# Every eighth block of a dense expert pass multiplied whole in float32, in place of a three-term product of two rounded parts

## The chip, the cores and the metric

The kernel runs on one core of one Trainium2 chip. The metric is the device time of one execution in microseconds. The core has a matrix engine (TensorE, PE in the profile, its weight loads PEld), a vector engine (VectorE, DVE), a scalar engine (ScalarE, ACT), GpSimd (POOL, which here mostly issues gathers), and SyncE (SP, which here issues nearly all plain transfers, in order). Each engine works through its own instructions in order and waits for the others by semaphores.

## The reference

One decoder block over 512 tokens of 1024 channels: two gated token mixers, a product-key expert layer (PEER), a gate with per-layer embeddings and a final norm. Only the expert layer matters here. Each token chooses 128 of 16384 experts (8 heads, 16 each):

```python
hid = jax.nn.gelu(jnp.einsum('td,thkd->thk', xb, tab_u[idx]))
return jnp.einsum('thk,thkd->td', gate * hid, tab_v[idx])
```

## The kernel before

Tokens are four tiles of 128. For tiles 0 and 1 the chosen rows of `tab_u` and `tab_v` are gathered one expert slot at a time (`Rows`, 128 rows of 4 KB in one indirect transfer) and worked on VectorE: a dot product at L789, a weighted addition into the tile at L793. Tiles 2 and 3 (`DENSE`, 256 tokens together) are done densely. A first pass (`products_of`, L904) multiplies the tokens with all 16384 experts in 128 blocks of 128 and leaves gate times gelu, a float32 matrix of 128 experts by 256 tokens a block, in `wide_w`; `place_of_block(j)` is the place of block j. A second pass, from about 1393 us on, multiplies these with the rows of `tab_v`: for block j a tile V of 128 experts by 1024 channels is loaded, and the product is added into four accumulators `acc[a, dh]` (two token tiles, two halves of the channels), each of 128 by 512, which stay in PSUM over all blocks.

The second pass is the one that matters. For block j, `split(j)` loads V by SP (L1054) and makes two parts of it and of the weights w: `Vh` (ACT, L1058) is V rounded to the reduced float32 type F32R, `Vl` (DVE, L1059) is the rest, also in F32R; `wh` (ACT, L1060) and `wl` (DVE, L1061) likewise, both in `w_parts`. `values(j, a)` then adds wh·Vh, wh·Vl and wl·Vh for each half: 2 x 3 x 2 = 12 matmuls a block on L1068, each of 128 by 128 weights and 512 moving columns.

What sets the order of the work:

- V has four places in turn: two buffers of the tag `V` (blocks with j % 4 of 0 and 1), and the rows of tiles 2 and 3 of `h` (j % 4 of 2 and 3), which are parked in DRAM for the pass (`rest`) and brought back at L1172. A place is used again four blocks on. SP issues the loads in order of j, so that a load that waits for its place holds back the loads behind it.
- `Vh` and `Vl` have two buffers each, taken in turn. `w_parts` has two places, by the parity of j.
- The four splitting instructions of a block are pinned to program order on ACT and DVE, and so are the gathers of `rows(PB)`: 0.96 expert rows a block of tile 1, each a gather from POOL (L762, five ring buffers `g`) and an addition on DVE (L793).
- Between the blocks, the last projection of the finished tiles is woven in: `finish(t, ...)` with its matmuls at L1094 (`pp`), L1102 and L1112 (`pg`). Its weights (`plew`, four loads of 1280 KB at L1147, and `fgain`, L1145) go into parts of `wide_w` that are no longer needed, and its other loads are at L1088.
- Blocks 126 and 127 are multiplied at the end, and the accumulators are added to `h` at L1179. What comes after that is the rest of `finish`.

In the trace the instructions of L1058 can be counted off from block 0 at 1392.53 us; block 71 is at 1598.81 us and block 119 at 1759.70 us. Float32 matmuls stand in the trace as two records each (2048 on L904 for 128 x 8 matmuls), F32R ones as one.

Of the kernel before, what the change touches and what calls it, by code (L numbers as in the profile page):

```python
# [60 lines left out]
def tile_block(ctx: ExitStack, tc: tile.TileContext, x, smalls, bvec, w1, w2, wbr, wout, wq, wup, gup, subk,  # L61
# [19 lines left out]
    def hrows(t):  # L81
        return first_h if t == 0 else later["h"][:, t - 1, :]
# [7 lines left out]
    def rank(n):  # L90

        tc.cur_priority = int(100000 * n)
# [127 lines left out]
    def pin(ins):  # L220

        return tc.keep_in_program_order(ins)
# [647 lines left out]
    def stream(name, tag):  # L870
        return dense.tile([128, D], F32, name=name, tag=tag, bufs=VS)
# [6 lines left out]
    def place_of_block(j):  # L878
        return wide_w[0][:, j, :] if j < N0 else wide_w[1][:, j - N0, :]
# [169 lines left out]
    halves_of = {}  # L1049

    def split(j):
        rank(9.5 + 0.001 * j)
        V = stream("V", "V") if j % 4 < 2 or j > 125 else hrows(j % 4)
        sp.dma_start(V, V3[:, j, :])  # L1054
        Vh = dense.tile([128, D], F32R, name="Vh", tag="uV", bufs=2)
        Vl = dense.tile([128, D], F32R, name="Vl", tag="X", bufs=VS)
        w, wh, wl = place_of_block(j), w_parts[:, j % 2, 0], w_parts[:, j % 2, 1]
        pin(act.activation(Vh, V, AF.Copy))  # L1058
        pin(dve.tensor_tensor(Vl, V, Vh, op=OP.subtract))  # L1059
        pin(act.activation(wh, w, AF.Copy))  # L1060
        pin(dve.tensor_tensor(wl, w, wh, op=OP.subtract))  # L1061
        halves_of[j] = wh, wl, Vh, Vl

    def values(j, a):
        wh, wl, Vh, Vl = halves_of[j]
        for q, (w, V) in enumerate(((wh, Vh), (wh, Vl), (wl, Vh))):
            for dh in range(2):
                pe.matmul(acc[a, dh], lhsT=w[:, a * 128:(a + 1) * 128], rhs=V[:, dh * 512:(dh + 1) * 512],  # L1068
                          start=j == 0 and q == 0, stop=j == 127 and q == 2)
# [62 lines left out]

    ends = {}
    split(0)
    for j in range(128):
        if j < 127:
            split(j + 1)
        rank(9.5 + 0.001 * j)
        rows(PB)
        if j < 126:  # L1140
            for a in range(2):
                values(j, a)
# [25 lines left out]
    for a in range(2):  # L1168
        for j in (126, 127):
            values(j, a)  # L1170
# [64 lines left out]
```

## Time and profile before

| what | value |
| --- | --- |
| median of 3 runs | 1846.44 us (1845.05 to 1847.0) |
| the profiled execution: its own time | 1847.93 us |
| its span | 1846.2 us |
| PE, DVE, ACT, POOL busy, share of the span | 90%, 78%, 35%, 43% |
| second pass, first matmul of L1068 to the last | 1393.9 to 1792.6 us |

The span is the time between the first and the last instruction of the profiled execution. The times that a row gives for a matmul include its way through the array; matmuls follow one another more closely than that, so that the cost of one is read from the distance between starts, or from a chain that names a run of them with its total.

### The profile page before, as it was taken

Reading aid. Unit: us, or ns where it says so; the run is one execution under the profiler, and the core shown is the slowest. Engines: PE = TensorE matmul, PEld = TensorE weight load, DVE = VectorE, ACT = ScalarE, POOL = GpSimd, SP = SyncE. Lnnn points to the kernel's source line nnn. Section 1 sums busy time; section 2 is a strip of 40 time slices with the busy share of each in tenths; the row PEclk is TensorE's granted clock in tenths of the full one; section 3 lists DMA queues with packets and bytes.
Section 4 is the critical chain, followed back from the end, with each engine's and each line's share of the span. In section 5 each row is a group of like instructions: output and inputs, shape, how many; then the busy total and the mean of one; then the engine's idle time right before and its main releaser. Section 6 shows DMA issues by size and latency. Waiting matters only on the chain.

```text
span 1846.2 us, 26873 instructions
## 1 busy us (share of the span) xinstructions
PE 1659.5 (90%) x9367; PEld 1481.7 (80%) x9367; DVE 1437.5 (78%) x3195; ACT 642.1 (35%) x1456; POOL 801.4 (43%) x608
## 2 busy tenths in 40 slices
PE   7999888999999889949970799999999999999997
PEld 6998878999898878948860689998887777888886
DVE  4532887887878899988627788988998999998773
ACT  3311233233222324401110454544433444454443
POOL 1000344343355465763004666655564554664220
PEclk9999988999999999979995899999999999999999
DMA  8257658556678987994430699999999999999750
GB/s 308 81 168 266 229 188 285 189 182 201 199 248 301 342 311 271 318 382 148 156 128 0 238 380 387 385 376 360 368 370 350 407 393 400 378 367 329 231 172 34
DMA packets 141851, 499.62 MB, mean 271 GB/s; under 512 B 15694, under 2 KB 20884, under 8 KB 141204
## 3 DMA queue, kind: packets, MB, share of 16 engines
q0 software_dynamic: 73728, 268.47, 40.0%
q1 hardware_dynamic: 67328, 228.09, 34.4%
q8 instruction: 74, 1.21, 0.3%
q10 hardware_dynamic: 660, 1.35, 0.2%
q14 instruction: 61, 0.50, 0.1%
HBM read 494.70 MB, written 3.15 MB: 270 GB/s over the span
## 4 chain that ended last, share of the span: by engine, by line
PE 53%; DVE 14%; issue 11%; DMA 11%; POOL 8%; ACT 1%; POOLq 0%; DVEq 0%; ACTq 0%; SPq 0%
PE S L904 14%; PE acc L1068 10%; POOL g L762 5%; PE z L273 5%; DMA g<-in_peer_u_dram,idx 5%; DMA g<-in_peer_v_dram,idx 3%; PE pg L1112 3%; PE pgate L273 3%; PE Z L458 2%; DVE g L789 2%; PE TT L465 2%; POOL sel L729 2%; DVE w L256 2%; PE pq L273 2%; PE cb L988 1%
## 5 line engine op out<-in xcount | busy, mean ns | idle before, releaser
L904 PE MATMUL S<-uT,U 128*128 128x256 f32 x2048 | 459.0, 383 | 26.5 <-ACT w L916 23.6
L762 POOL DMA_INDIRECT g<-in_peer_v_dram,idx x241 | 354.3, 1470 | 294.1 <-DVE h L793 223.2
L904 PEld LDWEIGHTS S<-uT,U 128*128 128x128 f32 x2048 | 388.1, 192 | 78.2 <-ACT w L916 24.0
L762 POOL DMA_INDIRECT g<-in_peer_u_dram,idx x235 | 298.9, 1272 | 248.9 <-DVE g L789 185.2
L793 DVE SCALAR_TENSOR_TENSOR h<-g,coef,h 128x1024 f32<-128x1024 f32 x241 | 308.3, 1279 | 15.1 <-DMA g<-in_peer_v_dram,idx 14.4
L789 DVE SCALAR_TENSOR_TENSOR g<-g,u 128x1024 f32<-128x1024 f32 x235 | 281.8, 1222 | 40.0 <-DMA g<-in_peer_u_dram,idx 39.4
L1068 PE MATMUL acc<-Vh,w_parts 128*128 128x512 f32 x1024 | 285.4, 397 | 5.6 <-ACT w_parts L1060 3.3
L1068 PEld LDWEIGHTS acc<-Vh,w_parts 128*128 128x128 f32 x1024 | 193.0, 189 | 50.3 <-ACT w_parts L1060 5.4
L1068 PE MATMUL acc<-Vl,w_parts 128*128 128x512 f32 x512 | 161.6, 397 | 1.7 <-DVE Vl L1059 1.7
L729 POOL TENSOR_TENSOR sel<-sel 128x800 f32<-128x800 bf16 x32 | 60.2, 1898 | 181.0 <-DVE sel L728 164.3
L1068 PEld LDWEIGHTS acc<-Vl,w_parts 128*128 128x128 f32 x512 | 96.3, 190 | 26.0 <-DVE Vl L1059 5.4
L273 PE MATMUL z<-xh,w 128*128 128x384 f32 x416 | 91.3, 364 | 17.4 <-DVE w L256 8.7
L1058 ACT ACTIVATE Vh<-V 128x1024 fp32r<-128x1024 f32 x66 | 70.0, 1061 | 96.8 <-PE acc L1068 73.6
L1059 DVE TENSOR_TENSOR Vl<-V,Vh 128x1024 fp32r<-128x1024 f32 x66 | 80.8, 1224 | 21.6 <-ACT Vh L1058 21.5
L1058 ACT ACTIVATE Vh<-h 128x1024 fp32r<-128x1024 f32 x62 | 65.8, 1061 | 89.1 <-PE acc L1068 73.2
L273 PEld LDWEIGHTS z<-xh,w 128*128 128x128 f32 x416 | 78.4, 202 | 22.2 <-DVE w L256 9.5
L1059 DVE TENSOR_TENSOR Vl<-h,Vh 128x1024 fp32r<-128x1024 f32 x62 | 76.0, 1226 | 19.1 <-ACT Vh L1058 19.0
L1000 ACT ACTIVATE w<-cb 128x156 f32<-128x156 f32 (+36 forms) x95 | 22.6, 271 | 174.6 <-DVE w L998 171.5
L916 ACT ACTIVATE w<-S 128x256 f32<-128x256 f32 (+41 forms) x123 | 38.1, 314 | 112.0 <-PE S L904 109.4
L988 PEld LDWEIGHTS cb<-h 128*128 128x128 f32 x512 | 67.8, 191 | 10.6 <-ACT h L983 4.0
L988 PE MATMUL cb<-h 128*128 128x128 f32 x512 | 70.1, 277 | 4.7 <-ACT h L983 2.5
L983 ACT ACTIVATE h<-near,gain 128x128 f32<-128x128 f32 x128 | 63.2, 493 | 4.3
(343 smaller groups left out, 2881.0 us busy)
## 6 DMA issues: line engine op xcount, KB each, us to landing
U<-in_peer_ut_dram SPq DMA_DIRECT2D x128, 512.0 KB, 6.3
V<-in_peer_v_dram SPq DMA_DIRECT2D x66, 512.0 KB, 6.5
h<-in_peer_v_dram SPq DMA_DIRECT2D x62, 512.0 KB, 6.4
w1b<-in_w_dram SPq DMA_DIRECT2D x52, 512.0 KB, 5.2
w2m<-in_w_dram SPq DMA_DIRECT2D x32, 512.0 KB, 4.4
wqb<-in_wq_dram SPq DMA_DIRECT2D x32, 512.0 KB, 5.1
wbr<-in_wbr_dram SPq DMA_DIRECT2D x16, 512.0 KB, 4.5
wo<-in_wout_dram SPq DMA_DIRECT2D x16, 512.0 KB, 5.5
```

The costliest lines, as they stand in the source:

```text
L273: pe.matmul(p, lhsT=a(c), rhs=b(c), start=k + c == 0, stop=(k, c) == (len(terms) - 1, n - 1))
L729: pool.tensor_tensor(hit, eq, ci[:, hd, None, :].to_broadcast([128, 16, NCAND]), op=OP.mult)
L762: fetch = pool.indirect_dma_start(out=g, out_offset=None, in_=tab, in_offset=bass.IndirectOffsetOnAxis(ap=ix[:, k:k + 1], axis=0))
L789: done = dve.scalar_tensor_tensor(g, g, 1.0, self.u, op0=OP.mult, op1=OP.mult, accum_out=self.dots[:, hd, k:k + 1])
L793: done = dve.scalar_tensor_tensor(h, g, self.cf[:, k:k + 1], h, op0=OP.mult, op1=OP.add)
L904: done = pe.matmul(p, lhsT=U[:, c * 128:(c + 1) * 128], rhs=uT[c // 4][:, c % 4, :], start=c == 0, stop=c == KC - 1)
L983: pin(act.activation(B[:, q], near, AF.Relu, scale=of(self.minus), bias=of(self.gate)))
L988: pin(pe.matmul(self.p[:, q, :], lhsT=As[:, t4 % 2, q], rhs=Bs[:, t4 % 2, q], start=True, stop=True))
L1058: pin(act.activation(Vh, V, AF.Copy))
L1059: pin(dve.tensor_tensor(Vl, V, Vh, op=OP.subtract))
L1068: pe.matmul(acc[a, dh], lhsT=w[:, a * 128:(a + 1) * 128], rhs=V[:, dh * 512:(dh + 1) * 512], start=j == 0 and q == 0, stop=j == 127 and q ...
L1112: pe.matmul(p[:, :256], lhsT=hT[:, c, :], rhs=plew_s[qd][:, c, :], start=(c == 0), stop=(c == KC - 1))
```

## The change

Blocks with j % 8 == 7 below 126 (7, 15, ..., 119: fifteen of the 128) are not split. Their w and V stay float32 tiles, and one float32 product takes the place of the three F32R products. The accumulators and all other blocks are as they were.

```diff
@@ def split(j):
         rank(9.5 + 0.001 * j)
         V = stream("V", "V") if j % 4 < 2 or j > 125 else hrows(j % 4)
         sp.dma_start(V, V3[:, j, :])
+        if j % 8 == 7 and j < 126:
+            halves_of[j] = place_of_block(j), V
+            return
         Vh = dense.tile([128, D], F32R, name="Vh", tag="uV", bufs=2)
@@ def values(j, a):
-        wh, wl, Vh, Vl = halves_of[j]
-        for q, (w, V) in enumerate(((wh, Vh), (wh, Vl), (wl, Vh))):
+        terms = [halves_of[j]]
+        if len(terms[0]) == 4:
+            wh, wl, Vh, Vl = terms[0]
+            terms = [(wh, Vh), (wh, Vl), (wl, Vh)]
+        for q, (w, V) in enumerate(terms):
             for dh in range(2):
```

## Rows read from the trace of the kernel before

**Rows 1.** Page, part 2: the span in 40 slices, busy tenths.
```profile
PE   7999888999999889949970799999999999999997
DVE  4532887887878899988627788988998999998773
DMA  8257658556678987994430699999999999999750
```

**Rows 2.** Busy time (us) by stretch of the second pass, clock, DMA share, GB/s.
```profile
1400.00:1545.00 145.00, 141.97 (x602) 113.19 (x601) 131.85 (x148) 68.27 (x100) 76.70 (x47) 0.99 1.00 386
1545.00:1690.00 145.00, 145.00 (x637) 118.49 (x636) 137.42 (x153) 73.39 (x114) 84.73 (x53) 1.00 0.99 371
1690.00:1784.00 94.00, 92.87 (x415) 77.08 (x413) 71.63 (x87) 43.60 (x77) 25.23 (x24) 1.00 0.77 253
```

**Rows 3.** Chain that ended last, 1540 to 1680 us: start, us, what.
```profile
1540.89 132.32 PE acc L1068 x574
1673.21 1.73 PE pp L1094 x8
1674.94 2.77 PE acc L1068 x12
```

**Rows 4.** Waits, 1400 to 1690 us: total us, times, longest.
```profile
ACT Vh L1058 <- PE acc L1068: 117.8, 82, 5.2
...
PE acc L1068 <- ACT w_parts L1060: 1.6, 3, 0.9
PE acc L1068 <- DVE Vl L1059: 1.4, 5, 0.5
```

**Rows 5.** Timeline, blocks 71 and 72: start, us, engine, line, what.
```profile
1599.90 1.23 DVE L1059 TENSOR_TENSOR Vl<-h,Vh 128x1024 fp32r<-128x1024 f32 x1
...
1601.05 0.42 DVE L1061 TENSOR_TENSOR w_parts<-w,w_parts 128x256 fp32r<-128x256 f32 x1
1601.16 0.33 SPq L1054 DMA_DIRECT2D h<-in_peer_v_dram  x1
1601.38 1.28 DVE L793 SCALAR_TENSOR_TENSOR h<-g,coef,h 128x1024 f32<-128x1024 f32 x1
1601.55 1.06 ACT L1058 ACTIVATE Vh<-V 128x1024 fp32r<-128x1024 f32 x1 [1.38 <-PE acc L1068]
...
1602.52 0.40 ACT L1060 ACTIVATE w_parts<-w 128x256 fp32r<-128x256 f32 x1
1602.65 1.23 DVE L1059 TENSOR_TENSOR Vl<-V,Vh 128x1024 fp32r<-128x1024 f32 x1
...
1604.30 1.06 ACT L1058 ACTIVATE Vh<-V 128x1024 fp32r<-128x1024 f32 x1 [1.38 <-PE acc L1068]
```

**Rows 6.** Chain in the first pass, 1028 to 1060 us.
```profile
1034.54 3.46 PE S L904 x16
```

**Rows 7.** Timeline of PE, 61 to 66 us: two records of one float32 matmul.
```profile
62.48 1.02 PE L416 MATMUL pb<-am,bones 128*128 128x512 f32 x2
63.34 1.05 PE L421 MATMUL pg<-zw,gup_s 128*128 128x128 f32 x8
```

**Rows 8.** Timeline of SP and ACT, 1450 to 1472 us.
```profile
1452.54 0.42 SPq L1147 DMA_DIRECT2D w<-in_plew_dram  x1
1454.96 3.13 SPq L1054 DMA_DIRECT2D V<-in_peer_v_dram  x2
...
1466.01 1.06 ACT L1058 ACTIVATE Vh<-V 128x1024 fp32r<-128x1024 f32 x1 [3.64 <-DMA V<-in_peer_v_dram]
1468.58 1.06 ACT L1058 ACTIVATE Vh<-V 128x1024 fp32r<-128x1024 f32 x1 [1.20 <-DMA V<-in_peer_v_dram]
1471.14 1.07 ACT L1058 ACTIVATE Vh<-h 128x1024 fp32r<-128x1024 f32 x1 [1.20 <-DMA h<-in_peer_v_dram]
```

**Rows 9.** DMA issues: count, KB, median us to landing; 1545 to 1690, then 1700 to 1750 us.
```profile
h<-in_peer_v_dram SPq DMA_DIRECT2D x25, 512.0 KB, 6.3
...
h<-in_peer_v_dram SPq DMA_DIRECT2D x6, 512.0 KB, 4.4
```

**Rows 10.** Line L1054: transfers of the whole pass, issue to landing.
```profile
DMA to landing us min/median/max: 3.3/6.4/11.0
```

## The prediction

> **What bounds the kernel now.** I read the slices of the page first: from the thirtieth on, the second pass, PE, DVE and the DMA engines all stand at 8 or 9 tenths, so the slices don't say which of the three is the bound [rows 1]. Busy time by stretch says more: from 1545 to 1690 us PE is busy 145.00 of 145 us, DVE 137.42, DMA share 0.99; from 1400 to 1545 PE lacks 3.0 us; after 1690 DVE (71.63 of 94) and DMA (0.77) have room and PE has not [rows 2]. The granted clock is 0.99 to 1.00, the level of 2.4 GHz. The chain that ended last runs through 574 matmuls of L1068 in one piece, 132.32 us, or 230.5 ns for each and 2.77 us for a block of 12; the same 2.77 us stands later, where DVE has room [rows 3]. The waits agree: ACT waits 82 times for PE to free a Vh buffer, 117.8 us in all, while PE waits for ACT or DVE only 3.0 us, in eight places [rows 4]. So **PE sets the pace of the second pass**, block for block; the splitting on ACT and DVE runs ahead of it and is held back by it. DVE is a near second: in a block it gives about 1.15 us to Vl, 0.33 to wl, 1.27 to the gathered row, by the distances of their starts, 2.75 us in all [rows 5].
>
> **What is removed.** In 15 blocks, ACT's 1.06 + 0.40 us and DVE's 1.23 + 0.42 us [rows 5]: some 22 us of ACT and 25 us of DVE. As both wait for PE, this is worth nothing by itself. On PE 12 matmuls of 230.5 ns go: 2.77 us a block [rows 3].
>
> **What is added on PE.** Four float32 matmuls of 512 columns a block. The trace has no such matmul in this pass, but it has two neighbours. In the first pass a block is 8 float32 matmuls of 256 columns, 16 records: the same 2048 moving columns, and with float32 weights and PSUM sums as here. It takes 3.46 us [rows 6]. And one float32 matmul of 512 columns, early in the kernel, keeps PE for 63.34 - 62.48 = 0.86 us with its two records; four of them are 3.44 us [rows 7]. The two agree, and I take 3.45 us: a block gets longer by 3.45 - 2.77 = **0.68 us**, fifteen by **10.2 us**. The bounds are 0.67 and 0.69 a block, 10.0 to 10.4 us.
>
> The Trainium skill has a rule that speaks against the change: on its page "FP8 and Floating Point Precision", section "TensorE Precision Notes", true float32 takes four passes through the array, and the reduced kind reads four bytes and truncates. If each pass cost what a reduced matmul costs here, a block would be 16 x 230.5 ns = 3.69 us in place of 12, and fifteen would cost 13.8 us, an estimate from that rule and [rows 3]; the measured 0.86 us for one matmul is 3.7 such passes, so the rows come out a little cheaper than the rule, and I go by the rows.
>
> **What is moved: when V's place comes free.** Before, V of block 71 was read for the last time by Vl, which ended at 1599.90 + 1.23 = 1601.13 us, and SP issued the load into this place (block 75's) at 1601.16 [rows 5]. Now PE itself reads V until the block ends. PE's blocks end when ACT's next Vh starts: Vh of block 72 at 1601.55 was released by the end of block 70, Vh of block 73 at 1604.30 by the end of block 71 [rows 5]. So the load of block 75 is issued at about 1604.3 + 0.68 = 1605.0, **3.8 us later**, and behind it in SP's order wait the loads of blocks 76 and 77, and any other load of SP that falls there. Who waits for that: Vh of block 75, due when block 73 ends, two blocks of 2.75 us after block 71, so 5.5 us after the new issue. Landing takes 6.3 us in the middle there, with the load before it still under way, 4.4 where the DMA has room, and 3.3 at least [rows 9, 10]. Here the queue of V has had nothing new for 3.8 us, so I take 4.4 to 5.5. If it does come late, there is cushion: wh of block 72 is done at 1602.92 and Vl at 1603.88 for a block that starts at about 1604.3 and needs Vl only with its third matmul, 0.46 us on, so that 0.9 us of lateness stay unseen by PE [rows 5]. The loads behind it follow at the queue's own spacing: after one of the 1280 KB loads three late blocks became ready 2.57 and 2.56 us apart, at full DMA share [rows 8], less than PE's 2.75 us. **I take this at nothing.** Even the usual landing of 6.3 us would be late by 0.8, inside the cushion. The lower bound is 0, as an issue that comes later can't help; the upper one is the first rival's price.
>
> The buffers of Vh, Vl skip a turn, so that the next block's split may start one block earlier; wh keeps its place by parity and still waits for the block two before. Nothing on PE waits for it. The start and stop marks of the accumulators stay where they were, no cost.
>
> **What is hidden.** PE's eight gaps, 3.0 us in all, lie in the stretch before 1545 us, where PE is busy 141.97 of 145 us [rows 2, 4] and late loads set the pace for a while: two loads issued from 1454.96 us on, behind a 1280 KB load, are ready at 1466.01 and 1468.58 [rows 8]. There a longer block lets the DMA catch up. Six changed blocks (7 to 47) lie in this stretch and bring 6 x 0.68 = 4.1 us, enough to fill all 3.0 if each stood ahead of a gap; the later issue of one load in eight takes some of it away. I take the middle, 1.5 us; bounds 0 and 3.0.
>
> **The sum:** 10.2 + 0 - 1.5 = **+8.7 us**. The profiled execution took 1847.93 us (span 1846.2), which would become 1856.6; it lies 1.5 us above the median, and on the median of 1846.44 us the forecast is **1855.1 us**. After the pass nothing changes: the last changed block is 119, at 1760 us, and what follows the accumulators only starts later.
>
> **The rivals.**
>
> *The late loads stall PE (slower still).* If the loads of blocks 75, 76 and 77, issued close together, share the queue rather than take turns, the first lands when the last does. With two of them that is 2 x 2.56 us + 1.8 (4.4 less one service of 2.56) = 6.9 us, less 5.5 and the cushion of 0.9: 0.5 us a block; with three, 9.5, or 3.1 us a block. It would bite where the queue is not backlogged anyway, in the nine changed blocks from 55 on: 4.5 to 28 us more, 1859.5 to 1883, middle 1868. For it: DMA share 0.99 [rows 2]. Against it: the even spacing of late blocks, which is that of loads that take turns [rows 8]. Chance 0.12.
>
> *The pass hides it (no change).* If the DMA and not PE sets the pace, the longer block comes out of waiting time, and the time stays within 0 to +3.5 us, 1846.4 to 1850, middle 1848. For it: DMA share 1.00 to 0.99 until 1690 [rows 2]. Against: PE waits only 3.0 us in that stretch, so there is no more to hide in [rows 4]. Chance 0.06.
>
> *Float32 is cheap here (faster).* The point is a record of 2.77 / 8 = 346 ns: if the eight float32 records of a block follow each other faster than that, PE gains. At the 230.5 ns of an F32R matmul the block would be 1.84 us, fifteen would give back 13.9 us: 1832.5. The place is L1068 alone. Against it stand both neighbours, 430 ns a record [rows 6, 7]; for it only that the early row is one matmul in another surrounding. Chance 0.03. That freed DVE time speeds up the pass is the weaker form of it: DVE lacks room only where PE lacks it more [rows 2]. Chance 0.02, some -4 us, 1842.
>
> **How the numbers follow.** The forecast has 0.77. Its own range is 10.0 - 3.0 = +7.0 to 10.4 + 0.9 = +11.3, so 1853.4 to 1857.7; with the spread of the runs and about 1 us for SP's order, 1852 to 1859. The range reaches into the nearest part of the stall: 1851.5 to 1864. A measurement of this kernel tells about 0.2%, 3.7 us, from no change. Slower by more: the forecast, the stall, 0.90. Within: the hidden case with a rest of the forecast, 0.06. Faster: 0.04.
>
> **What would show it.** Each step has its row in the profile after: L1068 with 120 float32 records (15 x 8) at some 592 ns each or a distance of 0.43 us, and a chain with 3.4 to 3.5 us for eight of them; the second pass longer by 8 to 10 us from its first matmul to its last; ACT's and DVE's splitting down to 113 of 128, and their busy time down by 22 and 25 us, with no gain; SP's load four blocks after a changed one waiting for PE instead of DVE, 3.8 us later than the rhythm; PE's idle time before L1068 no more than the 3.0 us of now. The prediction is wrong if the eight records take less than 3.2 or more than 3.7 us, if PE's idle time in the pass grows by more than 3 us (the stall), or if it stays and the pass is no longer than before (hidden).

## The result and the profile after

The changed kernel takes **1898.78 us** (median, 1893.1 to 1905.98) against 1845.89 us before: a ratio of 1.0297 (95% interval 1.0267 to 1.0328), 53 us slower by the medians, 55 by the ratio. The forecast was 1855.1 with a range to 1864. The direction was right; the size was too small by a factor of six.

The profiled execution took 1897.22 us, span 1895.4. From the last matmul of the accumulators to the end it is 53.5 to 53.6 us in both kernels, and the second pass starts 2.1 us earlier, so all of the difference lies in the pass: from its first matmul to its last 398.7 us before (1393.9 to 1792.6), 450.1 after (1391.8 to 1841.9). Busy time by stretch, in the columns of [rows 2] (PE, PEld, DVE, ACT, POOL busy, clock, DMA share, GB/s):

```profile
1400.00:1545.00 145.00, 131.26 (x495) 97.41 (x494) 106.63 (x117) 51.00 (x75) 54.95 (x40) 0.94 0.92 337
1545.00:1690.00 145.00, 132.93 (x499) 97.93 (x498) 108.16 (x119) 52.87 (x78) 59.11 (x42) 0.94 0.86 310
1690.00:1784.00 94.00, 92.62 (x391) 72.57 (x390) 67.45 (x81) 39.20 (x70) 35.15 (x30) 1.00 0.81 285
```

Where PE lacked 3.0 us in the first stretch and nothing in the second, it now lacks 13.7 and 12.1, the DMA share has fallen from 1.00 and 0.99 to 0.92 and 0.86, and the mean granted clock from 0.99 and 1.00 to 0.94. Nothing is the bound any more for the whole of these stretches: something makes all of them wait. The waits from 1400 to 1760 us (total us, times, longest) name it; they answer to [rows 4]:

```profile
ACT Vh L1061 <- PE acc L1074: 136.4, 53, 4.9
...
ACT Vh L1061 <- DMA h<-in_peer_v_dram: 54.7, 11, 6.7
...
PE acc L1074 <- ACT w_parts L1063: 25.5, 11, 4.0
```

Eleven times ACT waits for a load into `h`, 5 us each, and eleven times PE waits for ACT behind it. Before, ACT's waits for these loads were short, 1400 to 1690 us:

```profile
ACT Vh L1058 <- DMA h<-in_peer_v_dram: 11.7, 8, 2.6
```

SP's own rows around block 63, a changed one, show which load it is (start, us, engine, line, what):

```profile
1603.67 0.33 SPq L1054 DMA_DIRECT2D h<-in_peer_v_dram  x1
1607.66 0.33 SPq L1054 DMA_DIRECT2D V<-in_peer_v_dram  x1
1608.04 0.56 SPq L1094 DMA_DIRECT2D w<-in_pT_dram  x1
1610.32 0.34 SPq L1054 DMA_DIRECT2D V<-in_peer_v_dram  x1
1610.75 12.96 SPq L1054 DMA_DIRECT2D h<-in_peer_v_dram  x3
```

The places tell the blocks: h at 1603.67 is block 66, the two V are blocks 68 and 69, and only then comes h at 1610.75, block **67**, the one that had to wait for PE to finish with block 63. Before, a block's load was issued when Vl four blocks earlier was done, and that happened in the order of the blocks [rows 5]; SP's rows of the kernel before, blocks 74 and 75, then 76 and 77:

```profile
1598.41 3.07 SPq L1054 DMA_DIRECT2D h<-in_peer_v_dram  x2
1603.90 3.07 SPq L1054 DMA_DIRECT2D V<-in_peer_v_dram  x2
```

The program leaves unpinned transfers to the planner, the part of the kernel language that puts the instructions of each engine in order before anything runs. The orders seen here fit a planner that goes by when it reckons a place comes free, though its reckoning stands in no trace: with V of block 63 held by PE, the places of 68 and 69 come free first. So block 67, the next one needed, stands third in the queue. What that makes of the pass, ACT and then PE, some 10 us on:

```profile
1621.04 1.06 ACT L1061 ACTIVATE Vh<-h 128x1024 fp32r<-128x1024 f32 x1 [6.67 <-DMA h<-in_peer_v_dram]
...
1622.45 1.22 PE L1074 MATMUL acc<-Vh,w_parts 128*128 128x512 f32 x2 [3.99 <-ACT w_parts L1063]
1623.47 1.16 PE L1074 MATMUL acc<-Vl,w_parts 128*128 128x512 f32 x2
1624.42 1.91 PE L1074 MATMUL acc<-Vh,w_parts 128*128 128x512 f32 x4
```

The load takes from 1610.75 to about 1621.0, 10.2 us; PE stands still for 3.99 us, and when it goes on its matmuls follow one another every 0.43 to 0.5 us, in place of 0.23. This is the longest of the waits: in the thirteen turns whose late load no work of the last projection hides, the load is ready 7.5 to 10.3 us after its issue, 8.6 in the middle, and PE waits in twelve of them, 2.2 us in the mean. The clock says why the matmuls are slow (busy time and clock of three stretches, columns as above):

```profile
1622.40:1626.40 4.00, 3.95 (x9) 2.91 (x10) 4.00 (x6) 1.25 (x3) 1.25 (x1) 0.50 0.43 134
...
1566.90:1570.30 3.40, 3.40 (x8) 2.35 (x9) 3.40 (x5) 1.02 (x2) 0.88 (x1) 0.50 0.57 196
...
1597.60:1604.00 6.40, 6.40 (x29) 5.24 (x29) 5.46 (x7) 2.73 (x4) 2.65 (x3) 1.00 0.86 297
```

After nine of the twelve waits the granted clock falls to 0.50, the level of 1.2 GHz, for 3 to 7 us; in a stretch of steady work it is 1.00, the level of 2.4 GHz.

So the 51.4 us of the pass are, by this execution: fifteen longer blocks, 10.5 (below); PE's waits before the accumulators' matmuls, 28.8 against 3.3 us from 1398 to 1850 us, 25.5; and some 15 left over, in which PE works at the lower clock: a mean of 0.94 over the 290 us to 1690 is about 17 us of work lost, an estimate from the rows above.

### The profile page after: what moved, and what is told of

Read it like the earlier page. It is cut to its first block, busy times and chain, and to the rows that moved or that the text cites. A ratio compares the mean times of both kernels' runs of the same rounds, so it can differ in the third digit from the quotient of the medians.

```text
span 1895.4 us, 26650 instructions
## 1 busy us (share of the span) xinstructions
PE 1683.8 (89%) x9307; PEld 1477.1 (78%) x9307; DVE 1415.2 (75%) x3165; ACT 621.3 (33%) x1426; POOL 778.0 (41%) x608
## 4 chain that ended last, share of the span: by engine, by line
PE 51%; DVE 16%; DMA 12%; issue 11%; POOL 6%; ACT 4%; DVEq 0%; POOLq 0%; SPq 0%; ACTq 0%
PE S L904 16%; PE acc L1074 8%; DMA h<-in_peer_v_dram 5%; PE z L273 5%; PE pg L1118 3%; POOL g L762 2%; DVE h L793 2%; DMA g<-in_peer_u_dram,idx 2%; PE pgate L273 2%; DMA g<-in_peer_v_dram,idx 2%; PE Z L458 2%; PE TT L465 2%; PE cb L988 2%; DVE w L256 2%; POOL sel L729 2%
## 5 line engine op out<-in xcount | busy, mean ns | idle before, releaser
L762 POOL DMA_INDIRECT g<-in_peer_v_dram,idx x241 | 331.7, 1376 | 364.9 <-DVE h L793 285.9
L1074 PE MATMUL acc<-Vh,w_parts 128*128 128x512 f32 x904 | 272.1, 417 | 29.0 <-ACT w_parts L1063 28.6
L1074 PEld LDWEIGHTS acc<-Vh,w_parts 128*128 128x128 f32 x904 | 176.9, 197 | 79.3 <-ACT w_parts L1063 34.2
L1074 PE MATMUL acc<-Vl,w_parts 128*128 128x512 f32 x452 | 148.5, 411 | 2.2 <-DVE Vl L1062 2.2
L1062 DVE TENSOR_TENSOR Vl<-h,Vh 128x1024 fp32r<-128x1024 f32 x47 | 57.7, 1227 | 91.9 <-ACT Vh L1061 91.8
L1074 PEld LDWEIGHTS acc<-Vl,w_parts 128*128 128x128 f32 x452 | 88.1, 198 | 26.9 <-DVE Vl L1062 8.2
L1061 ACT ACTIVATE Vh<-h 128x1024 fp32r<-128x1024 f32 x47 | 49.8, 1059 | 153.4 <-PE acc L1074 93.0
```

The costliest lines, as they stand in the source:

```text
L762: fetch = pool.indirect_dma_start(out=g, out_offset=None, in_=tab, in_offset=bass.IndirectOffsetOnAxis(ap=ix[:, k:k + 1], axis=0))
```

## The experiments

Each is compared with runs of the kernel before on the same chip; the ratios carry 95% intervals. Two theories stood against each other: that the load behind a changed block comes late (because PE holds its place, or because of the order in which SP issues), and that float32 on PE costs more than its neighbours in the trace showed.

**Float32 without the hold (e1_copy).** ACT copies V of a changed block into a float32 tile in the turn of the Vh buffers, and PE reads the copy:

```diff
         if j % 8 == 7 and j < 126:
-            halves_of[j] = place_of_block(j), V
+            Vc = dense.tile([128, D], F32, name="Vc", tag="uV", bufs=2)
+            pin(act.activation(Vc, V, AF.Copy))
+            halves_of[j] = place_of_block(j), Vc
             return
```

> The changed kernel, but ACT copies V of a changed block to a float32 tile in a Vh buffer and PE reads that, so that V's place comes free as early as in the kernel before. If the 49 us of the changed kernel are late loads (V held until PE is done, and the granted clock lost after PE's waits), only the price of the eight float32 records is left, 15 x 0.66 to 0.69 us less what is hidden: 1853 to 1857 us, and PE idle in the pass no more than 3 to 4 us. The rival, that the float32 matmuls themselves slow the pass (through the clock or by a price that neighbours do not show), expects no recovery: 1885 to 1900 us, with the clock at half after each changed block.

Measured: 1850.52 against 1843.85 us, ratio 1.0034 (1.0012 to 1.0055), about +6.3 us by the ratio; the pass is 404.6 us long. The time lies 2.5 us below the range expected; the kernel before is some 2 us faster beside it. PE's waits from 1398 us on are 1.4 and 0.7 us. The float32 products are all there, and 48 of the 55 us are gone: the rival is out.

**The hold without float32 (e2_hold).** The kernel before, with a float32 matmul of two columns that reads V at the end of each eighth block:

```diff
+        if j % 8 == 7 and j < 126 and a == 1:
+            w, V = held_of[j]
+            pe.matmul(misc_ps("held")[:, 0:2], lhsT=w[:, 0:128], rhs=V[:, 0:2], start=True, stop=True)
```

> The kernel before, all blocks in three F32R terms, with one more float32 matmul of two columns at the end of each eighth block that reads V itself (its sum goes nowhere), so that V's place comes free only when PE is done. Late loads expect most of the 49 us without any float32 product: 1870 to 1890 us, PE idle in the pass at least 20 us. The rival, float32 itself, expects the two columns to cost some 0.1 us in 15 blocks: 1846 to 1849 us.

Measured: 1870.69 us, ratio 1.0133 (1.0087 to 1.0179); the profiled execution is the longest of the four, 1880.82 us, with a pass of 434.1 us and PE waits of 21.9. About 25 us without any float32 product: the lower end of what late loads expected. SP's rows show the order again, but less of it: the load that waits for PE stands behind one other, not two (blocks 58, 60, then 59).

```profile
1572.87 0.33 SPq L1054 DMA_DIRECT2D h<-in_peer_v_dram  x1
1578.36 0.33 SPq L1054 DMA_DIRECT2D V<-in_peer_v_dram  x1
1578.87 1.29 SPq L1054 DMA_DIRECT2D h<-in_peer_v_dram  x1
```

**The changed kernel with its loads in order (e3_pin_loads).**

```diff
-        sp.dma_start(V, V3[:, j, :])
+        pin(sp.dma_start(V, V3[:, j, :]))
```

> The changed kernel with the loads of V pinned on SP to the order of the blocks; in the changed kernel the load that waits for PE stands behind those of the two blocks after it (67 behind 68 and 69). If that order is what makes the load late, it lands first of its group and the cost falls to that of the float32 records: 1853 to 1860 us. If the later release alone makes it late, whatever the order, it stays at 1875 to 1900 us, and the loads behind it become late too.

Measured: 1854.97 us, ratio 1.0058 (1.0033 to 1.0082), about +10.7 us. On PE, DVE, ACT and POOL this kernel has the same instructions in the same order as the changed one; only SP differs. One pin takes back 44 of the 55 us. Its rows around block 71, whose float32 matmuls start at 1594.39 us (SP, then ACT, then PE):

```profile
1598.02 0.33 SPq L1054 DMA_DIRECT2D h<-in_peer_v_dram  x1
1598.44 0.90 SPq L1054 DMA_DIRECT2D V<-in_peer_v_dram  x2
```

```profile
1605.35 1.06 ACT L1061 ACTIVATE Vh<-h 128x1024 fp32r<-128x1024 f32 x1 [3.19 <-DMA h<-in_peer_v_dram]
1607.92 1.06 ACT L1061 ACTIVATE Vh<-V 128x1024 fp32r<-128x1024 f32 x1 [1.21 <-DMA V<-in_peer_v_dram]
```

```profile
1606.77 0.73 PE L1074 MATMUL acc<-Vh,w_parts 128*128 128x512 f32 x2 [0.52 <-ACT w_parts L1063]
```

The load is now first of its three and ready 7.3 us after its issue, and PE waits 0.52 us. This is again one of the longest: where ACT waits for such a load, it is ready after 5.9 to 7.5 us, 6.3 in the middle, against 8.6 in the changed kernel, and PE waits ahead of two late blocks, 0.52 and 0.66 us, where it waited ahead of twelve. The load also goes out sooner, 0.6 us after PE has begun the block behind the changed one; in the changed kernel it is 1.1, as it stands behind the load of block 69, which waits for its own place. The second load is ready 2.57 us after the first: loads of one queue are served in turn, as [rows 8] had it. The Trainium skill states on the page "DMA: Bandwidth & Descriptors", under "Queues, rings and completion order", that on each DMA engine the descriptors of a queue are taken in ring order, though a later one may finish its write first; the trace agrees as to the order, in which the loads here become ready. So the place in SP's order is a place in line.

**The pin alone (e5_before_pinned, e10_pinned_again).** The kernel before with the same pin.

> The kernel before with the loads of V pinned on SP to the order of the blocks, as a measure of the pin alone. Every theory expects no change: 1844 to 1849 us.

Measured: 1839.33 us, ratio 0.9978 (0.9956 to 1.0000), below the range expected and at the edge of a gain, so it was run again:

> The kernel before with the loads of V pinned, once more and with more rounds: it came out 4 us below the kernel before, at the edge of its interval. If that is the earlier start of the second pass (first matmul of the pass at 1387.8 us against 1393.9) it stays, 0.995 to 1.000 of the kernel before. If it was chance, 0.999 to 1.002.

Measured: 1842.57 against 1844.98 us, ratio 0.9991 (0.9969 to 1.0013). The pin by itself makes no difference in time that these runs can tell. The pass does start earlier in the traces of pinned kernels (1384.5 to 1390.2 us in six, against 1388.7 to 1395.1 in the six without the pin); why stays open, and some of what the pin takes back in e3_pin_loads may be of this kind, 2 to 4 us by these two ratios.

**The hold with the loads in order (e6_hold_pinned).** e2_hold and the pin.

> The kernel before with V of each eighth block held to the end of PE's block by a matmul of two columns, and the loads of V pinned to the order of the blocks. If the order on SP makes the load late and the hold alone does little, 1838 to 1848 us, some 25 us less than the hold without the pin (1870.7). If the hold is what costs, 1865 us or more.

Measured: 1848.44 us, ratio 1.0049 (1.0022 to 1.0077), some 9 us, or 11 to 13 above the pinned kernel before, where the hold without the pin cost 25. It is just above what the order expected, so the hold costs a little in order too. Part is the holding matmul itself: it puts off the next matmul by 0.14 us in the rows and the block by about 0.23, 3.4 us in all.

**The order alone (e7_order_alone).** The kernel before, no float32 and nothing held; the loads are pinned in the order of the changed kernel's SP:

```diff
-        V = stream("V", "V") if j % 4 < 2 or j > 125 else hrows(j % 4)
-        sp.dma_start(V, V3[:, j, :])
+        if j not in loaded:
+            for k in (j + 1, j + 2, j) if j % 8 == 3 and j > 8 else (j,):
+                loaded[k] = stream("V", "V") if k % 4 < 2 or k > 125 else hrows(k % 4)
+                pin(sp.dma_start(loaded[k], V3[:, k, :]))
+        V = loaded[j]
```

> The kernel before, no float32 product and no hold, with the loads of V pinned in the order that the changed kernel's SP has: the load four blocks after each eighth block stands behind those of the next two. If the order is the cause, that load waits for the place of the second of them, lands late as in the changed kernel, and 20 to 40 us come: 1864 to 1886. If a place held by PE is needed for the stall, 1838 to 1848 us.

Measured: **1903.11 us**, ratio 1.0350 (1.0300 to 1.0401). The whole loss of the change and more, from the order of the loads alone, and 17 us above the range expected. PE's waits from 1398 to 1850 us (total, times, longest) are longer than the changed kernel's 26.9; SP's rows show the same order:

```profile
PE acc L1071 <- ACT w_parts L1063: 43.9, 13, 5.5
```

```profile
1602.27 0.33 SPq L1056 DMA_DIRECT2D h<-in_peer_v_dram  x1
1607.76 0.33 SPq L1056 DMA_DIRECT2D V<-in_peer_v_dram  x1
1608.14 0.60 SPq L1091 DMA_DIRECT2D w<-in_pT_dram  x1
1610.51 0.34 SPq L1056 DMA_DIRECT2D V<-in_peer_v_dram  x1
1610.90 10.30 SPq L1056 DMA_DIRECT2D h<-in_peer_v_dram  x3
```

The waits come about in another way than in the changed kernel. The place of block 67 is free when Vl of block 63 ends, at 1604.99 us, but its load stands behind that of block 69, whose place is free at 1610.49. So it goes out 2.9 us after PE has begun block 64, in place of 1.1, and is then ready after 7.6 us (7.7 in the middle of thirteen turns), sooner than in the changed kernel. The run shows that this order is enough to make the load late with nothing held; it does not show how much of the changed kernel's loss is the late issue and how much the wait in line.

**Float32 alone, loads in order (e8_copy_pinned).** e1_copy and the pin.

> The changed kernel with V of a changed block copied by ACT (no hold) and the loads pinned: the float32 products alone. Against the pinned kernel before (1839.3) the records' price of 15 x 0.66 us, less up to 3 us of gaps that it fills: 1846 to 1850 us, and PE waits in the pass no longer than there. Were there more to float32 than its records, 1853 us or more.

Measured: 1846.14 us, ratio 1.0037 (1.0008 to 1.0067), beside 0.9978 and 0.9991 of the pinned kernel before: 0.5 to 0.6%, 8 to 11 us. Its rows give the price of a float32 block:

```profile
1571.00 0.62 PE L1076 MATMUL acc<-Vl,w_parts 128*128 128x512 f32 x2
1571.46 0.62 PE L1076 MATMUL acc<-Vh,w_parts 128*128 128x512 f32 x2
1571.92 3.60 PE L1076 MATMUL acc<-Vc,w 128*128 128x512 f32 x8
1574.96 1.03 PE L1076 MATMUL acc<-Vh,w_parts 128*128 128x512 f32 x2
1575.83 0.62 PE L1076 MATMUL acc<-Vl,w_parts 128*128 128x512 f32 x2
```

Without it the Vl matmuls would follow those of 1571.00 after two more pairs of 0.46 us each: from 1571.46 to 1575.83 are 4.37 us, less 0.92 are 3.45 us for the float32 block, against 2.75 for a split one. That is +0.70 us, 10.5 us for fifteen. (The start at 1574.96, ahead of the eighth record's end, is one of the modelled times.)

**PE kept at work through its wait (e9_after_busy).** The changed kernel with six float32 matmuls more ahead of the block that comes late; their sums go nowhere.

```diff
+        if j % 8 == 3 and 8 < j < 124 and a == 0:
+            p = misc_ps("busy")
+            for q in range(6):
+                pe.matmul(p[:, 0:256], lhsT=ident, rhs=place_of_block(j), start=True, stop=True)
```

> The changed kernel with six more float32 matmuls of 256 columns (2.6 us; their sums go nowhere) ahead of the block whose V comes late, so that PE works through most of its wait. If the clock that falls after those waits is part of the cost, it stays at its upper level (0.98 or more from 1400 to 1690 us against 0.94), and some 10 us come back, less what the extra matmuls outlast the waits: 1885 to 1895 us. If the clock costs nothing, the time stays at 1898 us or rises by up to 15 us.

Measured: 1893.23 us, ratio 1.0289 (1.0244 to 1.0334). PE's waits fall from 26.9 to 5.6 us, and the clock is back:

```profile
1400.00:1545.00 145.00, 140.17 (x549) 105.70 (x550) 106.38 (x118) 51.78 (x76) 54.74 (x40) 0.97 0.91 337
1545.00:1690.00 145.00, 142.74 (x577) 107.75 (x576) 113.10 (x125) 53.64 (x79) 63.66 (x44) 1.00 0.88 322
```

The time lies in the range that was expected if the clock is part of the cost, but the kernel before was 3 us faster beside it, and by its ratio the time isn't told apart from the changed kernel's. The trace, of the longest of the four executions (1904.33 us), shows two effects that cancel. From the first matmul of block 19 to that of block 91, nine turns with a late load each, it takes 239.4 us; the two traces of the changed kernel (the first one and that of e11_after_again) have 244.8 and 245.9. So 5 to 7 us come back. Behind block 91 the load is late by less or not at all, and the added work stands in PE's way, as ahead of block 99 (ACT, then PE):

```profile
1724.63 0.40 ACT L1063 ACTIVATE w_parts<-w 128x256 fp32r<-128x256 f32 x1
...
1727.07 2.75 PE L1071 MATMUL busy<-w,ident 128*128 128x256 f32 x12
...
1729.47 0.81 PE L1078 MATMUL acc<-Vh,w_parts 128*128 128x512 f32 x2
```

The parts of block 99 are ready at 1725.03 us, and its product starts when the added matmuls are through. From block 91 to the last matmul of the pass it takes 148.8 us, against 141.0 and 142.9. So the lower clock is part of the loss, by an estimate from these three traces some 5 to 7 us in nine turns; most of what is lost there stays with the kernel even at the full clock, as a turn still takes 26.6 us.

**The changed kernel again (e11_after_again)**, beside the same runs as e10.

> The changed kernel itself, beside the same runs of the kernel before as the pinned one: 1.027 to 1.033 again, and in the trace the same order of the loads and waits of PE of 25 to 35 us in the pass.

Measured: 1899.42 us, ratio 1.0295 (1.0267 to 1.0323), PE's waits 28.6 and 1.8 us, the same order on SP.

None of the kernels is faster than the one before by more than its interval; in a pass that PE sets, a block that costs PE 0.70 us more has no form that pays.

## Why the prediction was wrong

**What bounds the pass: right.** PE sets the pace as long as the loads keep up, and taking 20 us of busy time from ACT (642.1 to 622.0 in e3_pin_loads) and 23 from DVE (1437.5 to 1414.4) brought nothing.

**The price of float32: right.** 0.68 us a block forecast, from the two neighbours in [rows 6] and [rows 7]; 0.70 measured in e8_copy_pinned. The records are 120 of 592 ns, as foretold. The rule of four passes that the prediction cites from the Trainium skill ("FP8 and Floating Point Precision", "TensorE Precision Notes") gave 0.92 us by the prediction's estimate, 0.22 too dear here, as the rows had said.

**What is hidden, 1.5 us: not settled.** With loads out of the way, e1_copy is 6.3 us above the kernel before and e8_copy_pinned 8 to 11 us above the pinned one, around 10.5 less 1.5, but not sharper than that.

**When V's place comes free: here it failed.** The step named the right wait: V of a changed block is held until PE is done, and the load four blocks on comes later. Its issue was forecast 3.8 us late, and block 67's comes at 1610.75, 4.3 us after a block's distance of 2.75 us from that of block 66 (1603.67). What was wrong is the sentence on who waits behind whom. "Behind it in SP's order wait the loads of blocks 76 and 77" took the order seen in the trace of before for a rule of the program, as does the section on the kernel before. No line of the program fixes that order, and it moved with the places. The change made one place in eight come free late, and the planner put the loads of the next two ahead. A load that was thought first in an empty queue, 4.4 to 5.5 us, was third in a full one, and took 10.2 us. Against 5.5 us of time and 0.9 of cushion that is 3.8 us late, and PE's wait in that row is 3.99; with the middle landing of 8.6 it is 2.2, the mean of the twelve waits. The term that the prediction took at nothing measured 25.5 us of waits and some 15 of slow matmuls behind them.

Even in order the landing was forecast too short: 5.9 to 7.5 us in e3_pin_loads, 6.3 in the middle, with two loads close behind and the gathers beside it. The prediction had weighed 6.3 and found it inside the cushion, and PE's waits there bear it out but for two. That is the smaller error: e3 is 10.7 us above the kernel before, and e8, which holds nothing, 6.8 by its ratio, so the hold in order costs some 4 us, though their intervals overlap, or 6 to 10 by e6_hold_pinned less its own matmuls; the prediction had 0.

**The rivals.** The first, late loads that stall PE, had the right symptom, 0.12 of the chances and a top of 1883. Its mechanism was another (loads that share the queue; the runs show them served in turn), and it ended where it did because it reckoned with the order of the blocks. The range cut it off at 1864. The hidden pass and a cheap float32 are both out.

**The clock.** The prediction named no loss of clock. After nine of the twelve waits, 1.5 to 4.0 us long, the granted clock is 0.50 for 3 to 7 us; the three others, 1.2 to 1.5 us, and in the kernel before the longest wait within the pass, 0.9 us [rows 4], left it at 1.00. e9_after_busy, which keeps the clock, has some 5 to 7 us of it back in nine turns. The wait and the slow matmuls after it lie within one loop: load, split, product, release, next load into the same place.

**The loop.** Changed blocks sit eight apart and share one place with the blocks between them, so that a late load makes the next release late. In the changed kernel the first matmuls after the waits come at 1456.11, 1484.18, 1511.70, and on to 1700.90 us, 27.2 us apart in the mean of nine, where eight blocks took 22. The sum of a turn fits: 1.1 us from PE's start on the next block to the issue, 8.6 for the load, about 1.4 for Vh and wh, four split blocks of 2.75 and one of 3.45 make 25.6, and the slower matmuls the rest.

## What to carry to other kernels

Ask of a change that holds a buffer longer not only who waits for it but in which order the next loads will then be issued: an order in the trace that nobody wrote down can move with the release times, as it did here. Where the next load needed is the one whose place comes free last, pin the order, or copy the tile so that the place comes free early: here of 55 us the pin took back 44 and the copy 48. The place in line is part of the price: first of three 6.3 us in the middle, third 8.6, in a pass whose slack was 6.4; the other part is that a load issued in order waits for the places of those ahead of it, as e7_order_alone shows.

## What the runs showed of the hardware

- A float32 matmul of 128 by 512 stands in the trace as two records, 0.43 us apart, 0.86 us in all; the F32R one takes 0.230 us. Three F32R products of 12 matmuls are 2.75 us, one float32 product of 4 is 3.45 us.
- Transfers that one engine queues are served in turn even when the DMA share is 0.9 to 1.0: 512 KB loads issued together became ready 2.57 us apart.
- After nine of twelve waits of 1.2 to 4.0 us PE worked for 3 to 7 us at a granted clock of 0.50, and after one of 0.9 us at 1.00. Filling the waits with idle matmuls kept the clock at 0.97 to 1.00 and took 5 to 7 us off 245; where the load wasn't late, the idle matmuls cost as much again.
